# Powers of two of weight blocks from sums of squares on ScalarE in place of maxima on VectorE, asked for earlier

## The chip, the core and the metric

The kernel runs on one core of a Trainium2 chip. Its engines each work through a queue of their own, in order: TensorE (PE in the profile; PEld is its weight load), VectorE (DVE), ScalarE (ACT), GpSimd (POOL) and SyncE (SP), which here issues most of the transfers between the memory of the chip and the core. The metric is the time of one execution in microseconds of the device (us); lower is better.

## What is computed

A decoder block: normalisation, attention and a convolution side by side, gates, a projection, and then a SwiGLU feed-forward network (FFN) on 1024 tokens of width 1024 with a hidden width of 2816. The change concerns the FFN's first matrix:

```python
def swiglu_ffn(h, w_ffn_in, w_ffn_out):
    gate, up = jnp.split(h @ w_ffn_in, 2, axis=-1)
    return (jax.nn.silu(gate) * up) @ w_ffn_out
...
        x = x + rms_norm(merged @ w_mix_out[l], g_post_mix[l])
        h = rms_norm(x, g_pre_ffn[l])
        x = x + rms_norm(swiglu_ffn(h, w_ffn_in[l], w_ffn_out[l]), g_post_ffn[l])
```

## The kernel before

Every product is made in three passes, each operand split into a high and a low part (high x high, high x low, low x high). In the FFN's first matrix both parts are 16-bit floats, so a weight block has to be brought into their range first, by a power of two. `peaks` (line 122) finds the largest absolute value of each row of a block with DVE (L128), or of the two blocks of a pair, and joins them (L130, tile `pb`). `scales` (L133) sums these 128 values over the partitions with a one-column matmul against ones (L137), copies the sum (L140), keeps only its exponent (`power`, L120), and makes from it the factor `w` for the weights (L142, L143) and the factors `u` and `-u` that undo it in the results (L144, L145). With `w`, ACT casts the block to the high part (L239) and DVE makes the low part (L240); both are called from `quarters` or `part`.

The FFN has 22 hidden tiles of 128, each with a gate block and an up block of 128 x 1024 weights (`w_fi`). The first two tiles (`PLAIN`, in `ffn_half`) are computed in the plain way, four blocks with 24 matmuls of 512 columns for each half of the tokens. The other 20, j = 2 to 21, are pairs: `winograd` (L389) makes gate and up together in seven products (A11, A12, S2, S1, S3, S4, A22 of the weights) of 12 matmuls, 84 in all. After three matmuls comes a `tick`; a pair has 28. Three PSUM banks take the sums: X gets A11, is copied out (ACT, L398), gets S2 added, is copied out again (ACT, L403), and later gets S3 and A22 added; Z gets A12; V gets S1, is copied (ACT, L408), and gets S4. DVE joins these (L1816, L1821, L1825, L1829, L1838), and `sums` makes from two hidden tiles the Winograd sums for the next matrix and stores them (L1689 to L1701, transfers L1682): one difference and two stores at the end of an even tile, three and more at the end of an odd one.

While pair j is multiplied, the blocks of pair j+1 are prepared. `pair` (L337) writes this down in ticks from the pair's start: at LD = 2 SP issues the load of the two blocks (tiles `d` and `b`), at PK = 11 come `peaks`, at SC = 14 `scales`, at PC = 18, 20, 26 the first three of six `quarters`; the rest follow at 1, 8 and 10 in the next pair (8: casts of S3 and S4; 10: cast of A22). All engines take these steps into their queues at the place where they are called.

In the stage before, the projection `w_mx` (L1657) runs over eight token tiles, each followed by a residual and a norm (`residual`, `mix_norm`: squares L1344 and L1366, roots L1331, DVE L1351 and L1355, the normed tile L1368); four normed tiles are transposed (L1376). The pieces of work on the plain blocks stand in a list, of which one piece is done in every PIECE ticks; `weights` (L310) loads and lists blocks ahead, by `ahead` one further, and does at once what is still missing of the block that it hands out. 

Of the kernel before, what the change touches and what calls it, by code (L numbers as in the profile page):

```python
# [20 lines left out]
KT = 8  # L21
# [16 lines left out]

LD, PC = 2, (18, 20, 26)

PK, SC = 11, 14

TINY, W_TOP, H_TOP = 1e-22, 4096.0, 128.0

FIRST = 4

# [23 lines left out]
class Build:  # L70
# [51 lines left out]
    def peaks(self, i):  # L122

        nc = self.nc
        m = self.tiny(2, "pk", 4)
        raws = [self.raw[i - 1], self.raw[i]] if self.jobs[i][2] == "row2" else [self.raw[i]]
        for c, r in enumerate(raws):
            nc.vector.tensor_reduce(m[:, c:c + 1], r, AX.X, OP.max, apply_absolute_value=True)  # L128
        p = self.tiny(1, "pb", 4, BF16)
        nc.vector.scalar_tensor_tensor(p, m[:, 0:1], TINY, m[:, len(raws) - 1:len(raws)], op0=OP.max, op1=OP.max)  # L130
        self.peak[i] = p

    def scales(self, i):  # L133

        nc = self.nc
        ps = self.bank("s")
        nc.tensor.matmul(ps[:, 0:1], self.ones16, self.peak.pop(i), start=True, stop=True)  # L137
        t = self.tiny(4, "sc", 6)
        a, w, u, n = (t[:, c:c + 1] for c in range(4))
        nc.vector.tensor_copy(a, ps[:, 0:1])  # L140
        self.power(a, a)
        nc.vector.reciprocal(w, a)  # L142
        nc.vector.tensor_scalar(w, w, W_TOP, None, op0=OP.mult)  # L143
        nc.vector.tensor_tensor(u, a, self.unscale, op=OP.mult)  # L144
        nc.vector.tensor_scalar(n, u, -1.0, None, op0=OP.mult)  # L145
        self.scale[i] = w, u, n


    def bg(self, g):
# [102 lines left out]
    def quarters(self, i, c):  # L252


        nc = self.nc
        if c == 0:
            self.hl[i] = {}
        o = self.hl[i]
        r1, r2 = self.raw[i - 1], self.raw[i]
        a11, a12, a21, a22 = r1[:, :H], r1[:, H:], r2[:, :H], r2[:, H:]  # L260
        add = self.wsplit.tensor_tensor
        l, r = slice(0, H), slice(H, 2 * H)
        sw = self.scale[i][0] if i >= self.scaled else None
        if c == 0:
            h, w = self.both(r1, sw)
            o["A11"], o["A12"] = (h[:, l], w[:, l]), (h[:, r], w[:, r])
        elif c == 1:
            self.s12 = self.ring()
            add(self.s12[:, l], a21, a22, op=OP.add)
            add(self.s12[:, r], self.s12[:, l], a11, op=OP.add)  # L270
        elif c == 2:
            h, w = self.both(self.s12, sw)
            o["S1"], o["S2"] = (h[:, l], w[:, l]), (h[:, r], w[:, r])
        elif c == 3:
            self.s34 = self.slot()
            add(self.s34[:, l], a11, a21, op=OP.add)
            add(self.s34[:, r], self.s12[:, r], a12, op=OP.add)
# [59 lines left out]
    def pair(self, i):  # L337
# [8 lines left out]
        if n < len(J) and J[n][2] == "row1":  # L346
            todo += [(LD, lambda: self.load_ahead(n + 1))]
            if n >= self.scaled:
                todo += [(PK, lambda: self.peaks(n + 1)), (SC, lambda: self.scales(n + 1))]
            todo += [(k, lambda c=c: self.quarters(n + 1, c)) for c, k in enumerate(PC)]  # L350
            if self.conv_sums:
                todo.append((22, self.channel_sum))
            self.queued = n + 2
# [1035 lines left out]
    def norm_scale(self):  # L1389

        nc = self.nc
        self.ones16 = self.small.tile([128, 128], BF16, name="ones16")
        nc.vector.memset(self.ones16, 1.0)
        g = self.row_gain(self.g_pref_row)
        t = self.small.tile([128, 3], F32, name="nsc")
        a, b, self.unscale = (t[:, c:c + 1] for c in range(3))
# [6 lines left out]
        nc.vector.tensor_scalar(self.unscale, a, 1 / (H_TOP * W_TOP), None, op0=OP.mult)  # L1403
# [10 lines left out]
def build(ctx, tc, aps):  # L1414
    B = Build(ctx, tc, aps)
# [229 lines left out]
    for tiles in ((0, 1), (2,), (3,), (4,), (5,), (6,), (7,)):  # L1645
        banks = {tt: (B.bank(), B.bank()) for tt in tiles}
        for kt in range(KT):
            if len(W) == kt:
                B.ahead = int(kt < KT - 1)
                W.append(B.weights(mx[kt]))  # L1650
            for tt in tiles:
                m = mop[tt // 4]
# [22 lines left out]
        B.finish(e)  # L1675


    B.PIECE = 4
    held = {}

    def spill(p, name, x):
# [365 lines left out]
```

## Time and profile before

| | |
|---|---|
| median of three runs (lowest, highest) | 1740.39 us (1739.18, 1743.83) |
| the profiled execution | 1745.37 us |
| its span in the profile | 1743.6 us |
| DVE's maxima L128 | 44, each 1.21 us |
| PE's one-column matmuls L137 | 24, each 0.16 us |

Times in the profile are counted from the start of the span. A row of the order in time gives start, duration, engine, line, operation, output<-input by the program's names without numbers (`b`, `c`, `d` are buffers, `p` is PSUM, `sc` and `pb` the small tiles of the scales), and in brackets how long the engine was idle before it and who released it. A matmul's duration holds its way through the array, so neighbours overlap; what counts is the distance from start to start. SPq marks a transfer that SP issues, with the time to issue it.

### The profile page before, as it was taken

The page shows a single profiled execution, that of the slowest core. Times are in us where ns is not written, and L with a number is a line of the kernel's source. Part 1 is how long each engine was busy: PE and PEld are TensorE (multiplying, and loading weights), DVE is VectorE, ACT ScalarE, POOL GpSimd, SP SyncE. Part 2 cuts the span into 40 slices and gives each one's busy share as a digit, 9 for nine tenths or more (in the row PEclk, how much of TensorE's full clock was granted, in tenths as well). Part 3 has the DMA queues.
Part 4 walks back from the last instruction along what each step waited for, and adds up shares of the span by engine and source line. Part 5 has one row for each costly group of instructions (what it writes and reads, how often), then busy time and mean ns, then how long its engine had stood idle before and what let it go on. Part 6 is the DMA issues. An engine that isn't in the chain of part 4 may idle for free.

```text
span 1743.6 us, 24779 instructions
## 1 busy us (share of the span) xinstructions
PE 1692.8 (97%) x8722; PEld 1287.1 (74%) x8722; DVE 1317.8 (76%) x2438; ACT 806.4 (46%) x1552; POOL 494.9 (28%) x386
## 2 busy tenths in 40 slices
PE   8999999999999999999999999889999999999998
PEld 7788888888888999999888887434444444488886
DVE  6789988889997656686764855777777777767586
ACT  6343444343444566677622446633333333454453
POOL 0018778788884245455200300000000000000000
PEclk9999999999999999999999999999999999999999
DMA  4342434445678696878746722112332232394244
GB/s 162 112 170 91 151 124 138 161 170 174 189 180 225 211 286 175 226 222 235 242 169 228 267 76 82 67 73 91 119 117 91 91 126 92 133 355 159 89 147 151
DMA packets 159625, 277.58 MB, mean 159 GB/s; under 512 B 47009, under 2 KB 78428, under 8 KB 159500
## 3 DMA queue, kind: packets, MB, share of 16 engines
q1 hardware_dynamic: 155292, 263.82, 46.7%
q0 software_dynamic: 3920, 11.91, 2.1%
q8 instruction: 69, 1.13, 0.3%
q14 instruction: 56, 0.46, 0.1%
q10 hardware_dynamic: 288, 0.27, 0.0%
HBM read 185.34 MB, written 95.33 MB: 161 GB/s over the span
## 4 chain that ended last, share of the span: by engine, by line
PE 79%; DVE 10%; DMA 4%; ACT 3%; issue 2%; POOL 1%; SPq 0%; DVEq 0%; ACTq 0%; POOLq 0%
PE p L1930 12%; PE p L384 12%; PE p L385 12%; PE p L386 12%; PE p L1657 5%; PE p L368 4%; PE p L372 4%; PE p L370 4%; DVE pk L128 2%; PE p L1005 2%; PE p L1003 2%; PE p L1007 2%; PE p L617 2%; PE p L1101 2%; PE p L1137 1%
## 5 line engine op out<-in xcount | busy, mean ns | idle before, releaser
L384 PE MATMUL p<-b,b 128*128 128x512 f32 (+1 forms) x1124 | 433.9, 386 | 0.9 <-ACT c L398 0.7
L385 PE MATMUL p<-b,b 128*128 128x512 f32 (+1 forms) x1124 | 433.6, 386 | 0.0
L386 PE MATMUL p<-b,b 128*128 128x512 f32 (+1 forms) x1124 | 433.5, 386 | 0.0
L1930 PE MATMUL p<-b,b 128*128 128x512 f32 x924 | 209.8, 389 | 0.0
L1930 PEld LDWEIGHTS p<-b,b 128*128 128x128 f32 x924 | 173.4, 188 | 36.1
L747 DVE SCALAR_TENSOR_TENSOR p<-b,par,p 128x511 f32<-128x511 f32 (+14 forms) x232 | 163.4, 738 | 0.0
L368 PE MATMUL p<-b,b 128*128 128x512 f32 (+1 forms) x368 | 147.0, 399 | 0.0
L372 PE MATMUL p<-b,b 128*128 128x512 f32 (+1 forms) x368 | 146.4, 398 | 0.0
L370 PE MATMUL p<-b,b 128*128 128x512 f32 (+1 forms) x368 | 146.2, 397 | 0.0
L384 PEld LDWEIGHTS p<-b,b 128*128 128x128 f32 x644 | 120.9, 188 | 26.4 <-ACT c L403 0.7
L386 PEld LDWEIGHTS p<-b,b 128*128 128x128 f32 x644 | 120.9, 188 | 25.1
L385 PEld LDWEIGHTS p<-b,b 128*128 128x128 f32 x644 | 120.9, 188 | 24.9
L249 POOL TENSOR_TENSOR b<-d,b 128x1024 fp32r<-128x1024 f32 x44 | 106.8, 2428 | 79.9 <-ACT b L248 72.5
L1003 PE MATMUL p<-b,b 128*128 128x256 f32 x384 | 116.0, 302 | 0.0
L1005 PE MATMUL p<-b,b 128*128 128x256 f32 x384 | 115.2, 300 | 0.0
L1007 PE MATMUL p<-b,b 128*128 128x256 f32 x384 | 115.1, 300 | 0.0
L384 PEld LDWEIGHTS <-b 128*128 128x128 f16 x480 | 47.1, 98 | 75.6 <-issue 21.9
L1243 DVE TENSOR_TENSOR b<-c,b 128x512 fp32r<-128x512 f32 (+1 forms) x101 | 70.4, 698 | 35.3 <-ACT b L1242 35.0
L1242 ACT CAST b<-b 128x512 fp32r<-128x512 f32 (+1 forms) x117 | 72.3, 619 | 47.3 <-PE p L1930 18.0
L1243 DVE TENSOR_TENSOR b<-b,b 128x512 fp32r<-128x512 f32 (+1 forms) x117 | 80.0, 688 | 17.7 <-ACT b L1242 15.8
L386 PEld LDWEIGHTS <-b 128*128 128x128 f16 x480 | 47.2, 98 | 57.5 <-issue 1.4
L1657 PE MATMUL p<-b,b 128*128 128x512 f32 x384 | 89.6, 392 | 0.0
(272 smaller groups left out, 3526.1 us busy)
## 6 DMA issues: line engine op xcount, KB each, us to landing
b<-w_in SPq DMA_DIRECT2D x30, 512.0 KB, 4.8
dk<-c SPq DMA_DIRECT2D x48, 256.0 KB, 3.0
dq<-c SPq DMA_DIRECT2D x48, 256.0 KB, 3.7
b<-dq SPq DMA_DIRECT2D x48, 256.0 KB, 8.7
b<-dk SPq DMA_DIRECT2D x48, 256.0 KB, 6.2
b<-w_fi SPq DMA_DIRECT2D x24, 512.0 KB, 4.9
d<-w_in SPq DMA_DIRECT2D x23, 512.0 KB, 3.8
dqS<-c SPq DMA_DIRECT2D x44, 256.0 KB, 2.0
```

What stands on the lines that cost most here:

```text
L368: nc.tensor.matmul(ps, hi[:, s], a, start=kt == 0, stop=False)
L370: nc.tensor.matmul(ps, hi[:, s], b, start=False, stop=False)
L372: nc.tensor.matmul(ps, lo[:, s], a, start=False, stop=kt == nk - 1)
L384: nc.tensor.matmul(ps, hi[:, s], a, start=first and kt == 0, stop=False, skip_group_check=True)
L385: nc.tensor.matmul(ps, hi[:, s], b, start=False, stop=False, skip_group_check=True)
L386: nc.tensor.matmul(ps, lo[:, s], a, start=False, stop=kt == 3, skip_group_check=True)
L747: nc.vector.scalar_tensor_tensor(A[i][:, j:], src[i][:, :H - j], w[i], A[i][:, j:], op0=OP.mult, op1=OP.add)
L1003: nc.tensor.matmul(o, a, hi[:, s], start=kt == 0, stop=False)
L1005: nc.tensor.matmul(o, a, lo[:, s], start=False, stop=False)
L1243: nc.vector.tensor_tensor(s[:, 512:512 + n], src, f(s[:, :n]), op=OP.subtract)
L1657: nc.tensor.matmul(banks[tt][nh], st, wt[:, nh * H:(nh + 1) * H], start=bool(kt == 0 and a), stop=bool(kt == KT - 1 and b))
L1930: nc.tensor.matmul(acc[t], x, y, start=first and e == 0, stop=last and e == 2, skip_group_check=True)
```

## The change

`peaks` no longer takes maxima on DVE: ACT squares each block (times 2^-13) with the sum of each row as a by-product, into a tile that nobody reads (`junk`), and adds the two sums of a pair, or copies the one. The one-column matmul stays. `scales` then shifts the bits of the sum right by one and keeps the exponent, which halves the exponent (the power of two of a root), and makes `w`, `u` and `-u` in four small DVE operations instead of six. The steps in a pair come at other ticks: `peaks` at 9 instead of 11, `scales` at 16 instead of 14, and the three `quarters` at 19, 17, 25 instead of 18, 20, 26, so that the sums on DVE (quarter 1) go ahead of the first cast (quarter 0). For the plain blocks `ahead` is always 1, and PIECE is 2 instead of 4 until the pairs begin.

```diff
-PK, SC = 11, 14
-TINY, W_TOP, H_TOP = 1e-22, 4096.0, 128.0
+PK, SC, PS = 9, 16, (19, 17, 25)
+TINY, W_TOP, H_TOP = 2.0 ** -60, 2.0 ** -13, 128.0
...
         for c, r in enumerate(raws):
-            nc.vector.tensor_reduce(m[:, c:c + 1], r, AX.X, OP.max, apply_absolute_value=True)
+            nc.scalar.activation(self.junk, r, AF.Square, scale=W_TOP, accum_out=m[:, c:c + 1])
         p = self.tiny(1, "pb", 4, BF16)
-        nc.vector.scalar_tensor_tensor(p, m[:, 0:1], TINY, m[:, len(raws) - 1:len(raws)], op0=OP.max, op1=OP.max)
+        if len(raws) == 2:
+            nc.scalar.activation(p, m[:, 0:1], AF.Identity, bias=m[:, 1:2])
+        else:
+            nc.scalar.copy(p, m[:, 0:1])
...
-        nc.vector.tensor_copy(a, ps[:, 0:1])
-        self.power(a, a)
+        nc.vector.tensor_scalar(a.bitcast(I32), ps[:, 0:1].bitcast(I32), 1, 0x7F800000,
+                                op0=OP.logical_shift_right, op1=OP.bitwise_and)
+        nc.vector.tensor_scalar(a, a, 2.0 ** 64, TINY, op0=OP.mult, op1=OP.max)
         nc.vector.reciprocal(w, a)
-        nc.vector.tensor_scalar(w, w, W_TOP, None, op0=OP.mult)
-        nc.vector.tensor_tensor(u, a, self.unscale, op=OP.mult)
-        nc.vector.tensor_scalar(n, u, -1.0, None, op0=OP.mult)
-        self.scale[i] = w, u, n
+        nc.vector.tensor_scalar(u, self.unscale, a, None, op0=OP.mult)
+        self.scale[i] = w, t[:, 2:3], t[:, 3:4]
...
-            todo += [(k, lambda c=c: self.quarters(n + 1, c)) for c, k in enumerate(PC)]
+            todo += [(k, lambda c=c: self.quarters(n + 1, c)) for c, k in enumerate(PS if n >= self.scaled else PC)]
...
-                B.ahead = int(kt < KT - 1)
+                B.ahead = 1
...
-        B.ahead = 0
...
-    B.PIECE = 4
+    B.PIECE = 2
...
+    B.PIECE, B.ahead = 4, 0
```

In the changed file the lines behind L130 have other numbers: L131 and L133 are the new add and copy, L140 is the one-column matmul, L241 and L242 are the casts and low parts (L239 and L240 before).

The first place is ACT's queue in one pair (j = 4), from the first copy of X to the copy of V. Before (`c` on the left are the copies of PSUM, `b` and `c` with `sc` on the right are casts of weights):

```order
L398 COPY c_11882<-p_11880 128x512
L239 ACTIVATE b_11917<-b_11888,sc_11807 128x1024
L239 ACTIVATE c_11927<-b_11751,sc_11807 128x512
L403 COPY c_11883<-p_11880 128x512
L1818 ACTIVATE c_11882<-c_11882,sc_11807 128x512
L408 COPY c_11884<-p_11942 128x512
```

and after the change:

```order
L398 COPY c_11870<-p_11868 128x512
L241 ACTIVATE b_11905<-b_11876,sc_11803 128x1024
L128 ACTIVATE junk,pk_11912<-d_11882 128x1024
L128 ACTIVATE junk,pk_11912<-b_11884 128x1024
L131 ACTIVATE pb_11915<-pk_11912 128x1
L241 ACTIVATE c_11920<-b_11741,sc_11803 128x512
L403 COPY c_11871<-p_11868 128x512
L1820 ACTIVATE c_11870<-c_11870,sc_11803 128x512
L408 COPY c_11872<-p_11930 128x512
```

The two squares of the next pair's blocks and their sum have come between the cast for S3 and S4 and the cast for A22, ahead of the second copy of bank X (L403).

The second place is PE's queue around the one-column matmul of the same pair, with the engines that each row waits for. Before (V is `p_11942`, X is `p_11880`):

```order
L137 MATMUL p_11950<-pb_11936,ones_10348 128x1 [waits DVE_49]
L384 LDWEIGHTS b_11859
L384 MATMUL p_11942<-b_11476,b_11859 128x512
L385 LDWEIGHTS b_11859
L385 MATMUL p_11942<-b_11476,b_11859 128x512
```

and after (V is `p_11930`, X is `p_11868`):

```order
L386 MATMUL p_11930<-b_11498,b_11844 128x512
L140 LDWEIGHTS ones_10349
L140 MATMUL p_11944<-pb_11915,ones_10349 128x1 [waits Activation_49]
L384 LDWEIGHTS b_11905
L384 MATMUL p_11868<-b_11529,b_11905 128x512 [waits Activation_49]
```

Before, it stood in the middle of the product S1 into V; now it stands at that product's end, and the next matmul is the first of S3 into bank X, which waits for ACT.

The third place is ACT's queue at the plain blocks, around the norm of the last token tile (L1366 to L1368) and the transposed tokens (L1382). Before:

```order
L1707 ACTIVATE c_11135<-p_11136,sc_10493 128x512
L1366 ACTIVATE b_11196,ss_11197<-d_11140 128x1024
L1331 ACT_TABLE_LOAD
L1331 ACTIVATE rr_11199<-ss_11197,eps_rms 128x1
L1368 ACTIVATE b_11196<-d_11140,rr_11199 128x1024
L239 ACTIVATE b_11216<-b_11113,sc_11184 128x512 x2
L239 ACTIVATE b_11255<-b_11115,sc_11248 128x512 x2
L1382 ACTIVATE b_11273<-p_11268,gain_10403 128x512
```

and after:

```order
L241 ACTIVATE b_11183<-b_10500,sc_11170 128x512 x2
L1708 ACT_TABLE_LOAD
L1708 ACTIVATE c_11137<-p_11138,sc_10495 128x512
L1366 ACTIVATE b_11201,ss_11202<-d_11142 128x1024
L1331 ACT_TABLE_LOAD
L1331 ACTIVATE rr_11204<-ss_11202,eps_rms 128x1
L1368 ACTIVATE b_11201<-d_11142,rr_11204 128x1024
L128 ACTIVATE junk,pk_11215<-b_11131 128x1024
L133 CAST pb_11217<-pk_11215 128x1
L241 ACTIVATE b_11238<-b_11131,sc_11227 128x512 x2
```

The casts of the third plain block have gone ahead of the norm's L1366, and the square and copy for the fourth block stand right behind L1368. In PE's queue the one-column matmuls of the third and fourth block now stand 12 and 36 matmuls into the plain products, where the last three stood 0, 24 and 48 matmuls in.

More of the change, by code (lines that the diff above doesn't have):

```diff
@@ L138, in scales @@
         t = self.tiny(4, "sc", 6)
-        a, w, u, n = (t[:, c:c + 1] for c in range(4))
-        nc.vector.tensor_copy(a, ps[:, 0:1])
-        self.power(a, a)
+        a, w, u = t[:, 0:1], t[:, 1:2], t[:, 2:4]
+        nc.vector.tensor_scalar(a.bitcast(I32), ps[:, 0:1].bitcast(I32), 1, 0x7F800000,
+                                op0=OP.logical_shift_right, op1=OP.bitwise_and)
+        nc.vector.tensor_scalar(a, a, 2.0 ** 64, TINY, op0=OP.mult, op1=OP.max)
         nc.vector.reciprocal(w, a)
-        nc.vector.tensor_scalar(w, w, W_TOP, None, op0=OP.mult)
-        nc.vector.tensor_tensor(u, a, self.unscale, op=OP.mult)
-        nc.vector.tensor_scalar(n, u, -1.0, None, op0=OP.mult)
-        self.scale[i] = w, u, n
+        nc.vector.tensor_scalar(u, self.unscale, a, None, op0=OP.mult)
+        self.scale[i] = w, t[:, 2:3], t[:, 3:4]
     def bg(self, g):
@@ L255, in quarters @@
         nc = self.nc
-        if c == 0:
-            self.hl[i] = {}
-        o = self.hl[i]
+        o = self.hl.setdefault(i, {})
         r1, r2 = self.raw[i - 1], self.raw[i]
@@ L1391, in norm_scale @@
         nc = self.nc
+        self.junk = self.small.tile([128, 1024], BF16, name="junk")
         self.ones16 = self.small.tile([128, 128], BF16, name="ones16")
@@ L1394, in norm_scale @@
         g = self.row_gain(self.g_pref_row)
-        t = self.small.tile([128, 3], F32, name="nsc")
-        a, b, self.unscale = (t[:, c:c + 1] for c in range(3))
+        t = self.small.tile([128, 4], F32, name="nsc")
+        a, b, self.unscale = t[:, 0:1], t[:, 1:2], t[:, 2:4]
         yield 8
@@ L1402, in norm_scale @@
         nc.vector.tensor_scalar(b, b, H_TOP, None, op0=OP.mult)
-        nc.vector.tensor_scalar(self.unscale, a, 1 / (H_TOP * W_TOP), None, op0=OP.mult)
+        for c in range(2):
+            nc.vector.tensor_scalar(t[:, 2 + c:3 + c], a, (1 - 2 * c) / H_TOP, None, op0=OP.mult)
         self.gain2 = self.small.tile([128, 8], F32, name="gain2")
```

## The prediction

> **What bounds the kernel now.** I read the page first, then the view of waits for TensorE (PE), then the order in time around those waits.
>
> ```profile
> span 1743.6 us, 24779 instructions
> PE 1692.8 (97%) x8722; PEld 1287.1 (74%) x8722; DVE 1317.8 (76%) x2438; ACT 806.4 (46%) x1552; POOL 494.9 (28%) x386
> ```
>
> PE is busy for 97% of the span, so only time in which PE stands still, or runs at a lower clock, can be won. The view of waits (PE's line <- who released it: us in total, times, longest) says for whom it stands still:
>
> ```profile
> PE p L137 <- DVE pb L130: 28.3, 21, 5.5
> ```
>
> L137 is the one-column matmul that sums a block's peaks over the partitions. It stands in PE's queue among the large matmuls, so these wait with it until VectorE (DVE) has found the maxima. 28.3 us of such waits is 1.6% of the span, and the change works on just these. How they look in time is seen in two neighbouring hidden tiles (a "pair" below is one of the 20 passes of the Winograd loop; j=9, odd, then j=10, even):
>
> ```profile
> 1279.35 0.38 PE L384 MATMUL p<-b,b 128*128 128x512 f16 x1
> ...
> 1288.20 0.38 PE L386 MATMUL p<-b,b 128*128 128x512 f16 x1
> 1288.91 0.16 PE L137 MATMUL p<-pb,ones 128*128 128x1 bf16 x1 [0.33 <-DVE pb L130]
> 1288.94 0.38 PE L384 MATMUL p<-b,b 128*128 128x512 f16 x1
> ...
> 1298.00 0.38 PE L384 MATMUL p<-b,b 128*128 128x512 f16 x1
> ...
> 1306.85 0.38 PE L386 MATMUL p<-b,b 128*128 128x512 f16 x1
> 1308.53 0.16 PE L137 MATMUL p<-pb,ones 128*128 128x1 bf16 x1 [1.30 <-DVE pb L130]
> 1308.56 0.38 PE L384 MATMUL p<-b,b 128*128 128x512 f16 x1
> ...
> 1317.62 0.38 PE L384 MATMUL p<-b,b 128*128 128x512 f16 x1
> ```
>
> From 1279.35 to 1288.20 are 41 steps, 0.216 us each: 84 matmuls make 18.13 us. The odd pair takes 18.65 us, the even one 19.62: they lose 0.52 and 1.49, all at L137 (0.74 and 1.71 us from matmul to matmul, less one step). A stop costs 0.19 us more than the wait that is shown.
>
> **The change part by part: the pairs.** Of the waits, 16.0 us belong to the 18 pairs j=3 to 20, by this row less 5.47 and 5.32 us for two that are quoted below:
>
> ```profile
> PE p L137 <- DVE pb L130: 26.8, 20, 5.5
> ```
>
> (stretch from 1100 us on). With 18 x 0.19 us for the stops that is 19.4 us. DVE loses its two maxima and ScalarE (ACT) gets two squares with a sum; the one-column matmul moves from 14 ticks to 16 ticks after the pair's start (a tick is three matmuls, 0.65 us). Whether PE still waits depends on when the weight block lands, since the squares are asked for at tick 9, before it is there:
>
> ```profile
> 1301.03 0.32 SPq L1682 DMA_DIRECT2D dqS<-c  x1
> 1301.94 0.40 SPq L215 DMA_DIRECT2D b<-w_fi  x1
> 1281.97 0.40 SPq L215 DMA_DIRECT2D b<-w_fi  x1
> b<-w_fi SPq DMA_DIRECT2D x18, 512.0 KB, 4.7
> ```
>
> The last row is the list of DMA issues (count, size, median us to landing). In an even pair the load stands in SyncE's (SP) queue behind the stores of the last sums, which wait for DVE (the store at 1301.03 for L1701): it is issued 3.94 us after the pair's start and lands at 3.94 + 4.7 = 8.64. In an odd pair it is issued at 2.62 and lands at 7.32. The diff moves none of this, and DVE's last sums follow PE's last products as before.
>
> New durations by the nearest rows: a square with a sum over 128x1024 exists at L1366, a one-column add at L1331, and the two operations that come next in ACT's queue are old ones (idle time left as printed):
>
> ```profile
> 1076.56 1.06 ACT L1366 ACTIVATE b<-d 128x1024 f32<-128x1024 f32 x1 [3.52 <-DVE d L1355]
> 1077.74 0.30 ACT L1331 ACTIVATE rr<-ss,eps_rms 128x1 f32<-128x1 f32 x1
> 1302.30 1.15 ACT L239 ACTIVATE b<-b,sc 128x1024 f16<-128x1024 f32 x1 [0.92 <-DVE b L277]
> 1303.35 0.71 ACT L239 ACTIVATE c<-b,sc 128x512 f16<-128x512 f32 x1
> 1306.03 0.58 ACT L403 COPY c<-p 128x512 f32<-128x512 f32 x1 [1.97 <-PE p L386]
> 1306.51 0.72 ACT L1818 ACTIVATE c<-c,sc 128x512 f32<-128x512 f32 x1
> ```
>
> Even pair, in us from its start: second square starts at 8.67 (0.03 for the semaphore), its sum is there 1.15 later (L1366 starts at 1076.56, the operation on its sum at 1077.74, less 0.03): 9.82. The add, like L1331, ends 0.33 later: 10.15. PE sees it 0.06 later, an estimate from the 0.03 of other hand-overs: 10.21. The matmul's own turn is 16 ticks = 48 steps = 10.36. So **the wait for the peak goes**. But behind the squares in ACT's queue stand the cast of A22 (L239, 0.71) and the copy of bank X (L403, 0.58), which was done by 1306.61 - 1298.00 = 8.61 so far. PE's next product after the one-column matmul, S3, adds into the same bank X and has to wait for that copy. ACT's instructions overlap by 0.10 (1306.03 + 0.58 against 1306.51): the cast starts at 10.05, the copy at 10.66, it ends at 11.24, PE goes on at 11.30 instead of 10.39. **A new wait of 0.91 us takes the place of 1.49.** Odd pair: all of it 1.32 us earlier, 9.98 against 10.39: no wait, 0.52 won.
>
> That ACT keeps its order is seen above: the cast at 1303.35, whose input and scale were old, did not pass the L239 ahead of it that waited 0.92 us for DVE. The Trainium skill says so too ("TensorE: Matmul & The Clock Gate", section Architectural detail: the queues of ScalarE and VectorE are strictly first in, first out); by that the 0.91 us stay, and without it the first rival below would be the likelier one. No row speaks against it.
>
> Nine even pairs keep 9 x 0.91 = 8.2 us. Some blocks land late: these two lines of the chain of work (start, us) are 1.9 and 0.3 us over the median, the first in an odd pair:
>
> ```profile
> 1242.57 6.58 DMA b<-w_fi
> 1455.32 5.01 DMA b<-w_fi
> ```
>
> The first gives 9.98 + 1.9 - 10.39 = 1.5 us, the second 0.3 more. Together 10 us stay of 19.4: **9.4 us won.** Bounds: all 19.4, and below nothing (slower rival). DVE's half of A22 waits for the cast too, to 11.5, and the small scale steps behind it; what these feed is wanted only at the next pair's start at 18.1, so the wait is covered. DVE's relief (two maxima, two small steps) wins nothing in the pairs, where DVE is not what PE waits for once the peak is ACT's.
>
> **The first pair, j=2.** DVE is behind here, with the sums for the Winograd operands:
>
> ```profile
> 1141.98 0.38 PE L384 MATMUL p<-b,b 128*128 128x512 f16 x1 [0.70 <-ACT c L398]
> 1144.38 0.60 ACT L1242 CAST b<-b 128x512 f16<-128x512 f32 x1
> 1151.49 0.19 PE L137 MATMUL p<-pb,ones 128*128 128x1 bf16 x1 [5.47 <-DVE pb L130]
> 1151.92 0.63 PE L385 MATMUL p<-b,b 128*128 128x512 f16 x1
> 1157.40 0.38 PE L386 MATMUL p<-b,b 128*128 128x512 f16 x1
> ```
>
> PE loses 0.89 + 5.66 us (0.70 and 5.47 with 0.19 each), and after the long stop it runs at half speed: from 1151.92 to 1157.40 are 13 matmuls, 0.42 us each, 0.21 too much: 2.7 us. In all 9.2. The block has landed long before, so ACT can square it after the cast at 1144.38, from 1144.9 on; the second square starts at 1145.95, PE goes on 2.63 us later (the sum above) at 1148.6. Its turn without waits is about 1146.3 (it began its 42nd matmul at 1145.64 with 0.89 lost; seven steps more and 0.03, less 0.89). So at worst 2.3 us stay, if DVE and ACT are no sooner; none if they are 2.4 us sooner (two maxima of DVE are gone ahead of it, partly into idle time). I take 1.7: **7.5 us won**, between 6.9 and 9.2, a half-speed stretch not being due after so short a stop: after 1.30 us there is none (1308.53 to 1308.56).
>
> **The unpaired blocks** (two hidden tiles ahead of the pairs). Here the last token tile's norm stands in the same queues.
>
> ```profile
> 1084.65 0.57 ACT L1344 ACTIVATE d<-p 128x512 f32<-128x512 f32 x1
> 1089.22 0.18 PE L137 MATMUL p<-pb,ones 128*128 128x1 bf16 x1 [1.48 <-DVE pb L130]
> 1094.68 1.15 ACT L1368 ACTIVATE b<-d,rr 128x1024 f32<-128x1024 f32 x1 [0.87 <-DVE rr L1336]
> 1099.92 0.16 PE L137 MATMUL p<-pb,ones 128*128 128x1 bf16 x1 [5.32 <-DVE pb L130]
> 1102.46 0.73 PE L1376 MATMUL p<-ident,b 128*128 128x128 f32 x4
> 1103.03 0.38 PE L368 MATMUL p<-b,b 128*128 128x512 f16 x1
> ```
>
> After the change the square of the fourth block stands in ACT's queue behind L1368, the norm's last step. L1344, the norm's first step, can start when the last tile's matmuls are done, at about 1082.5 (the casts that stood ahead of it are made earlier), 2.15 us sooner. Into this come the third block's square and copy (1.15 + 0.33) and, between the norm's steps, its scale steps (four small ones, 0.7 by my estimate). The norm's end therefore stays where it is, L1368 at about 1094.7. Its successor starts 1.05 later; square 1.15 and copy 0.33: PE can go on at 1097.3. But its one-column matmul now stands 12 matmuls further ahead: 36 matmuls after 1082.4, at about 1090.4. **PE stands 6.9 us instead of 1.48 + 5.32 in two stops.** Half speed lasted from 1099.92 to 1103.03 there and from 1151.49 to 1157.3 in the first pair, 3.1 to 5.8 us, half of it lost: 1.5 to 2.9. The transposes, 18 matmuls on, then start at 1097.3 + 3.9 + (1.5 to 2.9) = 1102.7 to 1104.1, against 1102.46 and 0.36 us of slow transposes: 0 to 1.4 us lost, I take **0.7 lost**. The price of longer standing is bounded below by nothing and above by 2.9.
>
> The Trainium skill ("TensorE: Matmul & The Clock Gate", The HAM clock gate) has the clock halved after an idle window of about 3.4 us, and freed after as much work. The rows agree in kind (0.42 us steps after 5.3 and 5.5 us, none after 1.3); its 3.4 us would make this loss 1.7 us, an estimate, inside the 1.5 to 2.9.
>
> The rest costs nothing: ahead of this, two blocks' squares go to ACT, which is busy for less than half of the span, and one load goes ahead of the token loads, under matmuls that wait for nothing.
>
> **Sum.** 9.4 + 7.5 - 0.7 = 16.2 us. The profiled execution took 1745.37 us (span 1743.6 and 1.8 around it), the median of the runs is 1740.39; from that, **1724.2 us**, 0.93% less.
>
> **Rivals.**
> 1. *All waits of the pairs go*, because the copy of X is not late (a sooner landing by 0.9 us, from stores that clear sooner). Then 19.4 + 9.2 - 0.7 = 27.9: 1712.5 us. For it: the odd pairs have 0.4 us to spare already. Against: SP's load waits for DVE's last sum, which waits for PE.
> 2. *The peak's wait is only traded* for an equal one: blocks land 0.5 to 0.7 us later than the median. At 0.5, 9 x 1.41 + 9 x 0.09 + 1.8 = 15.3 stay and 4.1 are won, at 0.7 0.5; with 7.5 in the first pair and -2.9 in the unpaired blocks that is 8.7 to 5.1: 1732 to 1735 us. For it: the spread of the landings. Against: nothing new is transferred in the pairs.
> 3. *Slower*: the same wait on ACT, but at the late landing's price. While ACT waits for a block it holds the copy of X, which DVE's maxima never did. Landing x us later costs 9 (0.91 + x) in even pairs and 9 (x - 0.41) in odd ones. It eats 19.4 + 7.5 - 0.7 us from x = 1.2 on. If every block came as late as the one of 6.58 us (x = 1.9), 9 x 2.81 + 9 x 1.49 = 38.7 us of waits stand against 19.4: 1740.4 + 19.3 - 6.8 = 1753 us. For it: one block of 18 did. Against: the other 17.
> 4. *It does not do what it says*: the one-column matmul still waits as long, for ACT instead of DVE, in the first pair too. Then about 1740 us.
>
> **How the numbers follow.** Forecast 0.58 (1719 to 1730 by its own bounds), rival 1 0.17, rival 2 0.14, rival 3 0.05, rival 4 0.06. The likeliest gives the time. The range leaves out rivals 3 and 4 and the last of the first: 1711 to 1736. 0.3%, 5.2 us, is about what a measurement of this kernel can tell from no change. Faster by more than that: forecast, rival 1, and half of rival 2 and a little, 0.83; within it 0.11; slower 0.06.
>
> **What would show it.** In the changed profile: PE waits at S3's first matmul (L384) for ACT's copy L403, 0.9 us in even pairs and none in odd ones; next to none at the one-column matmul in the pairs; one stop of 6 to 7 us ahead of the transposes with slow matmuls behind it, and 1 to 2 us in the first pair. Odd pairs take 18.1 us, even ones 19.0. It is wrong if odd pairs stop too, if ACT's squares take more than 1.3 us each, or if the unpaired blocks' stop is over.

## The result: 0.73% less, and where it came from

| | before | after |
|---|---|---|
| median (lowest, highest), 5 runs each | 1740.39 us (1737.62, 1744.52) | 1727.75 us (1726.10, 1731.05) |
| ratio after / before, 95% interval | | 0.9927 [0.9906, 0.9948] |
| the profiled execution | 1745.37 us | 1729.81 us |
| its span | 1743.6 us | 1728.0 us |

In a later set of runs the changed kernel stood at 0.9916 [0.9902, 0.9930]. The page of the changed kernel, and its view of waits for PE (line, who released it: us in total, times, longest):

```profile
span 1728.0 us, 24733 instructions
PE 1692.5 (98%) x8722; PEld 1289.3 (75%) x8722; DVE 1256.7 (73%) x2323; ACT 860.4 (50%) x1664; POOL 495.8 (29%) x386
```

```profile
PE p L384 <- ACT c L403: 7.8, 11, 0.9
PE p L140 <- ACT pb L133: 6.1, 1, 6.1
...
PE p L1376 <- ACT b L1368: 1.7, 1, 1.7
...
PE p L384 <- DVE c L1823: 0.7, 1, 0.7
```

PE's busy time is what it was; its waits got shorter. The 28.3 us behind DVE's peak (L130) are gone, and four others stand there: for the copy of X (L403) in the pairs, for one square of a plain block (L133), in the projection for the norm's last step (L1368), and once, in the first pair, for DVE's L1823. Stage by stage, from the starts of PE's rows in the two profiled executions (us):

| stage | before | after | won |
|---|---|---|---|
| up to the projection | 990.98 | 991.00 | 0.0 |
| projection | 91.15 | 93.34 | -2.2 |
| plain hidden tiles | 53.80 | 54.29 | -0.5 |
| first pair, j=2 | 27.52 | 19.95 | 7.6 |
| the 19 pairs behind it | 363.67 | 353.00 | 10.7 |
| the second matrix, to the end | 216.48 | 216.45 | 0.0 |

**An odd and an even pair** in the changed kernel's order in time (start, duration, engine, line; in brackets the idle time before and the releaser), j=9 and j=10 as before:

```profile
1270.56 0.38 PE L384 MATMUL p<-b,b 128*128 128x512 f16 x1
...
1280.92 0.17 PE L140 MATMUL p<-pb,ones 128*128 128x1 bf16 x1
1280.95 0.38 PE L384 MATMUL p<-b,b 128*128 128x512 f16 x1
...
1288.71 0.38 PE L384 MATMUL p<-b,b 128*128 128x512 f16 x1
...
1299.08 0.17 PE L140 MATMUL p<-pb,ones 128*128 128x1 bf16 x1
1300.07 0.38 PE L384 MATMUL p<-b,b 128*128 128x512 f16 x1 [0.82 <-ACT c L403]
...
1307.83 0.38 PE L384 MATMUL p<-b,b 128*128 128x512 f16 x1
```

The odd pair takes 18.15 us, which is all matmuls. In the even one the one-column matmul no longer waits, and 19.12 us are left because the first matmul of S3 does. ScalarE's queue in the even pair shows for what:

```profile
1296.15 1.06 ACT L128 ACTIVATE junk<-d 128x1024 bf16<-128x1024 f32 x1 [2.05 <-DMA d<-w_fi]
...
1297.46 1.06 ACT L128 ACTIVATE junk<-b 128x1024 bf16<-128x1024 f32 x1 [0.16 <-DMA b<-w_fi]
...
1298.64 0.30 ACT L131 ACTIVATE pb<-pk 128x1 bf16<-128x1 f32 x1
1298.84 0.71 ACT L241 ACTIVATE c<-b,sc 128x512 f16<-128x512 f32 x1
1299.45 0.56 ACT L403 COPY c<-p 128x512 f32<-128x512 f32 x1
```

ACT stands twice for the landing of a block, then squares, adds and casts, and only then copies X, although the product that it copies was over by 1296.65. PE goes on 0.06 us after the copy's end.

**The projection.** On ACT, at the first token tile's norm and at the end of the fourth one's, and on PE at the transposes of these four:

```profile
1012.15 1.04 ACT L128 ACTIVATE junk<-b 128x1024 bf16<-128x1024 f32 x1
...
1013.32 0.19 ACT L133 CAST pb<-pk 128x1 bf16<-128x1 f32 x1
1013.42 0.59 ACT L1344 ACTIVATE d<-p 128x512 f32<-128x512 f32 x1
...
1048.04 1.15 ACT L1368 ACTIVATE b<-d,rr 128x1024 f32<-128x1024 f32 x1 [0.87 <-DVE rr L1336]
```

```profile
1049.23 0.33 PE L1376 MATMUL p<-ident,b 128*128 128x128 f32 x1 [1.68 <-ACT b L1368]
```

The square of the second plain block, now asked for one block ahead, stands in front of a norm's first step, and its scale steps and casts stand between later ones. ACT and DVE pass these norms to and fro, one tile behind the other, and nothing takes the delay up: the fourth tile's last step starts at 1048.04, where the kernel before has it at this time,

```profile
1045.74 1.15 ACT L1368 ACTIVATE b<-d,rr 128x1024 f32<-128x1024 f32 x1 [0.87 <-DVE rr L1336]
```

and its transposes wait 1.68 us.

**The plain tiles.** The one stop, and ScalarE's queue at its end:

```profile
1092.15 0.38 PE L372 MATMUL p<-b,b 128*128 128x512 f16 x1
1098.66 0.16 PE L140 MATMUL p<-pb,ones 128*128 128x1 bf16 x1 [6.13 <-ACT pb L133]
1098.69 0.59 PE L368 MATMUL p<-b,b 128*128 128x512 f16 x1
...
1103.34 0.45 PE L372 MATMUL p<-b,b 128*128 128x512 f16 x1
1103.62 0.38 PE L368 MATMUL p<-b,b 128*128 128x512 f16 x1
```

```profile
1096.20 1.15 ACT L1368 ACTIVATE b<-d,rr 128x1024 f32<-128x1024 f32 x1 [0.87 <-DVE rr L1336]
1097.26 1.04 ACT L128 ACTIVATE junk<-b 128x1024 bf16<-128x1024 f32 x1
...
1098.42 0.19 ACT L133 CAST pb<-pk 128x1 bf16<-128x1 f32 x1
```

The fourth block's square comes behind the norm's last step, and from 1098.69 on, PE makes a step in 0.43 us instead of 0.216 for almost 5 us.

### The profile page after: what moved, and what is told of

It reads as the page before. It is cut to its first block, busy times and chain, and to the rows that moved or that the text cites. A ratio compares the mean times of both kernels' runs of the same rounds, so it can differ in the third digit from the quotient of the medians.

```text
span 1728.0 us, 24733 instructions
## 1 busy us (share of the span) xinstructions
PE 1692.5 (98%) x8722; PEld 1289.3 (75%) x8722; DVE 1256.7 (73%) x2323; ACT 860.4 (50%) x1664; POOL 495.8 (29%) x386
## 4 chain that ended last, share of the span: by engine, by line
PE 82%; DMA 5%; DVE 5%; ACT 5%; issue 2%; POOL 1%; SPq 0%; DVEq 0%; ACTq 0%; POOLq 0%
PE p L384 13%; PE p L385 13%; PE p L386 13%; PE p L1932 12%; PE p L368 4%; PE p L372 4%; PE p L370 4%; PE p L1659 3%; DMA b<-w_fi 2%; PE p L1005 2%; PE p L1007 2%; PE p L1003 2%; PE p L617 2%; PE p L1101 2%; PE p L1137 1%
```

## The experiments

Twelve more runs were made (the last is the changed kernel again), in three sets, each with the kernel before on the same chip (its medians: 1742.0, 1743.17, 1742.5 us). The stretch ahead of the projection is the same code in all of them, and yet in the profiled executions it took between 983.6 and 993.3 us. So the readings below go by the stages behind it; the ratio stands beside them. These readings are of one execution each. The same kernel (after and e12) took 353.00 and 353.86 us in its 19 pairs.

| kernel | projection | plain tiles | first pair | 19 pairs | ratio to before, 95% interval |
|---|---|---|---|---|---|
| before | 91.15 | 53.80 | 27.52 | 363.67 | |
| after | 93.34 | 54.29 | 19.95 | 353.00 | 0.9927 [0.9906, 0.9948] |
| e1_copy_first | 93.37 | 54.06 | 20.77 | 370.11 | 1.0018 [1.0005, 1.0031] |
| e2_maxima_tick16 | 91.14 | 54.90 | 25.05 | 346.63 | 0.9903 [0.9885, 0.9922] |
| e3_old_pieces | 91.15 | 51.07 | 21.39 | 355.92 | 0.9906 [0.9887, 0.9924] |
| e4_old_ticks | 93.35 | 54.12 | 19.92 | 355.88 | 0.9938 [0.9921, 0.9956] |
| e5_pairs_late | 93.35 | 53.88 | 19.86 | 356.78 | 0.9940 [0.9926, 0.9954] |
| e6_pool_loads | 93.34 | 53.43 | 19.95 | 344.74 | 0.9866 [0.9846, 0.9885] |
| e7_front | 91.16 | 53.91 | 19.95 | 356.37 | 0.9909 [0.9891, 0.9928] |
| e8_both | 91.14 | 53.89 | 19.86 | 356.79 | 0.9928 [0.9912, 0.9944] |
| e9_before_pool | 91.15 | 54.92 | 26.39 | 362.32 | 0.9997 [0.9986, 1.0008] |
| e10_pool_old_pieces | 91.15 | 51.37 | 21.39 | 344.73 | 0.9846 [0.9829, 0.9864] |
| e11_pool_mx | 91.15 | 56.17 | 19.96 | 344.73 | 0.9867 [0.9852, 0.9881] |
| e12_after_again | 93.35 | 54.49 | 19.96 | 353.86 | 0.9916 [0.9902, 0.9930] |

### Squares behind the copy of X (e1)

```diff
-PK, SC, PS = 9, 16, (19, 17, 25)
+PK, SC, PS = 13, 16, (19, 17, 25)
```

> The kernel after the change, with the squares of the next pair asked for at tick 13 instead of 9, so that in ScalarE's queue they stand behind the second copy of bank X (L403) and no longer ahead of it; the one-column matmul stays at tick 16. Theory A (the new wait of PE in even pairs comes only from that place in the queue; the block is not later than before): the copy ends at 8.6 us after the pair's start, the squares begin as soon as the block lands (8.3 to 9.0), their sum is there at 9.9 to 10.6 against a turn at 10.4, so 0 to 0.2 us are left in even pairs. The changed kernel's waits at L384 for L403 in the pairs (6.7 us in 9 pairs, with 0.19 for each stop 8.4 us) go: 1727.75 - 8.4 + 1 = about 1720 us, even pairs 18.2 to 18.4 us. Rival B (the landing is what PE waits for, by whatever way): the wait moves to the one-column matmul L140 or, by the copy of bank V that now stands behind the squares, to the first matmul of S4, and even pairs stay at 19.0: 1727 us.

Neither: 1746.31 us, 0.2% slower than the kernel before, and every pair from the second on, odd or even, takes 19.57 us. ScalarE's queue in the even pair j=10 (start 1296.84), and PE behind it:

```profile
1304.81 0.58 ACT L403 COPY c<-p 128x512 f32<-128x512 f32 x1 [1.97 <-PE p L386]
1305.29 0.72 ACT L1820 ACTIVATE c<-c,sc 128x512 f32<-128x512 f32 x1
1305.92 1.04 ACT L128 ACTIVATE junk<-d 128x1024 bf16<-128x1024 f32 x1
...
1307.08 1.06 ACT L128 ACTIVATE junk<-b 128x1024 bf16<-128x1024 f32 x1
...
1308.26 0.30 ACT L131 ACTIVATE pb<-pk 128x1 bf16<-128x1 f32 x1
...
```

```profile
1308.61 0.16 PE L140 MATMUL p<-pb,ones 128*128 128x1 bf16 x1 [1.25 <-ACT pb L131]
```

The copy of X is on time and L403 is gone from the pairs' waits, as theory A said. But the expectation began the squares at the landing. Nothing in these rows waits for a landing: both squares now stand behind the copy and a Silu (L1820), where in the changed kernel the first is done before the second block is there. 3.8 us of work from the copy's start make 11.77 us after the pair's start, against a turn at 10.36.

### Maxima kept, only the ticks changed (e2)

```diff
-PK, SC = 11, 14
+PK, SC, PS = 11, 16, (19, 17, 25)
...
-            todo += [(k, lambda c=c: self.quarters(n + 1, c)) for c, k in enumerate(PC)]
+            todo += [(k, lambda c=c: self.quarters(n + 1, c)) for c, k in enumerate(PS if n >= self.scaled else PC)]
```

> The kernel before the change (maxima on VectorE, six small steps, old pieces), with only the ticks of the changed kernel behind the maxima: scales at 16 instead of 14, quarters at 19, 17, 25; maxima stay at 11. Theory A (in the pairs it is the later turn of the one-column matmul that wins the time, not the engine that makes the peak): in an even pair of the kernel before, the matmul ran at 10.53 us after the start and in an odd one at 9.56, against a turn that now comes at 10.4: odd pairs 18.15 us, even ones 18.2 to 18.5. 19.4 us of losses shrink to 2 or 3; the first pair's long wait shrinks by the 1.3 us of the later turn. 1740.4 - 17 - 1.3 = about 1722 us, so ahead of the change itself. Rival B (the move to ScalarE wins it): VectorE's six small steps and the first cast come 1.3 us later, the low parts behind them miss the next pair's start, and the waits come back there: 1735 us or more.

1725.55 us, theory A. The 19 pairs win 17.0 us, more than the 10.7 of the change itself: odd pairs take 18.15 us, even ones 18.32. Its view of waits from the second pair on has no row for PE. Over the whole kernel its ratio, 0.9903, and that of the change, 0.9927, have overlapping intervals. The first pair keeps its wait of 4.2 us and takes 25.05 us.

### The edits to the plain blocks' queue undone (e3)

```diff
-                B.ahead = 1
+                B.ahead = int(kt < KT - 1)
...
         B.PIECE = 3
+        B.ahead = 0
...
-    B.PIECE = 2
+    B.PIECE = 4
```

> The kernel after the change without its edits to the plain blocks' queue: one piece in 4 ticks again, and no block ahead on the last input tile of the projection. Theory A (these edits cost what the prediction had put at nothing): the squares of the second plain block no longer stand among ScalarE's norm steps of the fourth token tile, the 2.0 us that the transposes of the first four tiles waited go, and the stop of 6.1 us for the fourth block becomes one of 4.5 to 5.8 us: 1727.75 - 2 - 1 = about 1725 us (1723 to 1727). Rival B (the edits are what keeps the waits down to one stop): two stops again as before the change, 1730 us or more.

1727.14 us, at the edge of theory A's range, with one stop and not rival B's two. By its ratio it cannot be told from the changed kernel, so the stages have to say it. The projection is back at 91.15 us, the wait for L1368 is gone, the stop is 3.92 us long (the fourth block's one-column matmul has its turn 48 matmuls into the plain products again, instead of 36) and the plain tiles take 3.2 us less than after. The first pair takes 1.4 us more (its blocks are prepared later). The 19 pairs took 2.9 us more: 1.9 of them in one odd pair (j=7, 20.05 us), whose second square could start only 9.68 us after the pair's start instead of at about 7.3: PE waited 0.69 us for the peak and 0.92 for the copy. That is the price of a late landing that the third rival had named, in one pair of 19. It is there only without the block ahead on the last input tile, though why is not shown: in the five profiles without that block whose loads SP issues (before, e2, e3, e7, e8), transfers still run at 15 to 26 GB/s between 7.4 and 9.0 us after the start of j=7; in the five with it (after, e1, e4, e5, e12) none do. So these edits cost 5.4 us ahead of the pairs and give back 1.4 in the first and 1.9 in j=7.

### Squares with the old ticks (e4)

```diff
-PK, SC, PS = 9, 16, (19, 17, 25)
+PK, SC, PS = 11, 14, (18, 20, 26)
```

> The kernel after the change with the pair's old ticks: squares at 11, scales at 14, quarters at 18, 20, 26. It is ScalarE's squares without the new moments. Theory A: an even pair's peak is there at 10.2 us after the start as in the changed kernel, but the one-column matmul's turn is at 9.06: a wait of 1.15 us and 0.19 for the stop in nine even pairs; the copy of X is done before PE gets to S3, so the wait at L403 goes; odd pairs (peak at 8.9) wait for nothing. Even pairs 19.45 us instead of 19.1, odd 18.15; the first pair loses 1.3 us more: 1727.75 + 9 x 0.4 + 1.3 = about 1732.5 us. Rival B (the engine decides, the ticks are worth nothing): 1727 to 1728.5 us.

1731.43 us, theory A. From the second pair on there is one row of waits for PE,

```profile
PE p L140 <- ACT pb L131: 9.7, 9, 1.4
```

nine times in nine even pairs, and odd ones take 18.15. The first pair, 19.92 us, loses nothing by the old ticks; there the expected 1.3 us was wrong.

### Squares late and scales late (e5)

```diff
-PK, SC, PS = 9, 16, (19, 17, 25)
+PK, SC, PS = 13, 19, (20, 17, 25)
...
-        sw = self.scale[i][0] if i >= self.scaled else None
+        sw = self.scale[i][0] if i >= self.scaled and c != 1 else None
```

> The kernel after the change with squares at tick 13, as in the run with squares at 13 and scales at 16, but with scales at 19 and the quarters at 20, 17, 25. That earlier run's matmul ran at 11.77 us after the start of every pair, odd or even, early or late landing: copy of X (from 8.0), the Silu on the first sum (L1820), two squares and the add, one behind the other, 3.8 us. Theory A (that chain is all there is to it, and what comes behind the scale has time to spare): with its turn at 19 ticks = 12.31 us the matmul waits for nothing, the copy of X is not held, all pairs take 18.15 us: 8.4 us less than the changed kernel in nine even pairs, 1727.75 - 8.4 = about 1719.5 us. Rival B: the scale is now known 2 us later, the casts and low parts for the next pair come too late, and PE waits at the first product of the next pair (L384 or L386 for L241 or L242): 1725 us or more.

1734.14 us, in rival B's range, but at a place it did not name. From the second pair on the one-column matmul waits for nothing, and all these pairs take 18.82 us:

```profile
PE p L384 <- DVE c L1823: 9.2, 18, 0.5
```

```profile
1305.20 1.28 DVE L242 SCALAR_TENSOR_TENSOR b<-d,sc,b 128x1024 f16<-128x1024 f32 x1 [1.09 <-ACT b L241]
1306.40 0.68 DVE L1823 TENSOR_TENSOR c<-p,c 128x512 f32<-128x512 f32 x1
```

(The second edit lets quarter 1, the sums on DVE at tick 17, run before the scale is there; it does not use it.) The first row counts the pairs from the second on, the others are DVE's order in one of them. The first low part (L242) waits for a cast that waits for the scale, and holds up L1823, which reads bank X; the last product (A22) may add into X only after that. The scale cannot come as late as tick 19 while L1823 stands behind that low part.

### Loads from GpSimd's queue (e6)

```diff
-            self.nc.sync.dma_start(self.raw[j][:, :n], src)
+            (q or self.nc.sync).dma_start(self.raw[j][:, :n], src)
...
-            todo += [(LD, lambda: self.load_ahead(n + 1))]
+            todo += [(LD, lambda: self.load_ahead(n + 1, nc.gpsimd if n >= self.scaled else None))]
```

> The kernel after the change, with the loads of the next pair's blocks issued from GpSimd's queue instead of SyncE's, at the same tick 2. Theory A (in even pairs the blocks land 1.3 us later only because their load stands behind the stores of the last sums in SyncE's queue, and this landing is what holds the copy of X): loads are issued at 1.3 to 2.6 us in odd and even pairs alike, land at or under 7.5, even pairs take 18.15 us like odd ones, 1727.75 - 8.4 = about 1719.5 us. Rival B (it is not the place in SyncE's queue that makes them late, but buffers that come free late, or the stores' traffic): landing stays at 8.3 to 9.0 in even pairs and these stay at 19.0: 1727 us.

1720.44 us, theory A's time, and every pair from the second on takes 18.15 us; PE waits for nothing there. Two pieces of its order in time, GpSimd from the pair ahead on and ACT in the even pair j=10, which starts at 1285.71:

```profile
1270.98 0.53 POOL L217 DMA_DIRECT2D d<-w_fi  x1 [15.79 <-ACT c L398]
...
1290.46 0.53 POOL L217 DMA_DIRECT2D d<-w_fi  x1 [18.43 <-issue]
```

```profile
1291.00 1.04 ACT L128 ACTIVATE junk<-d 128x1024 bf16<-128x1024 f32 x1
...
1292.17 1.06 ACT L128 ACTIVATE junk<-b 128x1024 bf16<-128x1024 f32 x1
...
1294.16 0.56 ACT L403 COPY c<-p 128x512 f32<-128x512 f32 x1
```

The load at 1290.46 is for the next pair's squares; that at 1291.00 reads what was asked for at 1270.98, 20.0 us sooner. The expected 1.3 to 2.6 us was too late by a pair: GpSimd's queue has nothing else to do here and does not stay with PE's ticks. ACT no longer waits for a landing, and the copy of X starts at 8.45 us instead of 10.74.

### Another order on the plain blocks (e7), and both (e8)

```diff
-                B.ahead = 1
+                B.ahead = int(kt < KT - 1)
...
-    B.PIECE = 2
+    B.PIECE, B.ahead = 1, 1
...
         Ws.append((B.weights(fi[j][0]), B.weights(fi[j][1])))
+        if j == 0:
+            q, nop = list(B.pieces), (0, lambda: None)
+            B.pieces = deque((q[0], q[4], nop, nop, q[1], q[2], q[3], *q[5:]))
         ffn_half(j, 0, Ws[j])
+        B.PIECE = 2
```

> The kernel after the change, with another order of the work on the plain blocks and nothing else: no block ahead on the last input tile of the projection (as before the change), and at the start of the plain hidden tiles the squares of the third and fourth block first, one piece per tick, ahead of the last token tile's norm in ScalarE's queue, the scales from the fifth tick on. Theory A (the long stop is there because the fourth block's square stands behind the norm's last step L1368, and the wait in the projection because the second block's square stands among the norm steps): both go, with them the half-speed matmuls behind the stop; the norm ends one or two us later, which the transposes do not notice. 2.2 us of the projection, 6.3 us of stop and 2.3 us of half speed: 1727.75 - 10.8 = about 1717 us. Rival B (that norm is what PE waits for in the end): the stop moves to the transposes L1376, which wait for L1368 or its copies, and no more than 3 or 4 us are won: 1724 us.

1728.2 us; the ratio is 0.9909, against 0.9927 for the change in its own set. Rival B: the projection's 2.2 us are won, the stop for the fourth block is gone, and the plain tiles still take 53.91 us:

```profile
PE p L1376 <- ACT b L1368: 4.6, 1, 4.6
```

The transposes now wait for the last token tile's norm, which the squares and casts ahead of it have held up: its last step L1368 starts 16.6 us after the projection's last matmul, 4.7 us later than after the change. (The late landing in j=7, 20.01 us, takes back 1.9 us in this run's pairs, as in e3.) What PE waits for at this place is that norm, whichever instruction is the first to stand behind it. The second edit together with e5's:

> Both: squares at tick 13, scales at 19 and quarters at 20, 17, 25 in the pairs, and the new order on the plain blocks. Theory A of both holds and they add up, since the stages follow each other: 1727.75 - 8.4 - 10.8 = about 1708.5 us, 1.8% under the kernel before. If only one of them holds, 1717 to 1720 us.

1730.27 us. Its first stages are those of e7 and its pairs those of e5, to 0.1 us: they add up, as expected, but neither part brought what had been expected of it.

### The kernel before with loads from GpSimd's queue (e9)

The edit is that of e6, on the kernel before.

> The kernel before the change (maxima on VectorE, old ticks, old pieces), with the loads of the next pair's blocks issued from GpSimd's queue, as in the run that did this to the changed kernel, where they went out as soon as a buffer came free, about a pair ahead. It splits the 19.4 us that the pairs lost before. Theory A: 1.3 us of the late landing in each even pair goes, and the late one of the 18 loads; what an odd pair lost (0.52 us) stays in all, since VectorE's own order (low parts of the last blocks, then the maxima) lets the peak be ready 0.3 us after the turn at tick 14: 18 pairs of 18.65 us, 19.4 - 18 x 0.52 = 10 us won, 1743 - 10 = about 1732 us. Rival B (all of the loss is the landing): 18.15 us in all pairs, 1723 us. Rival C (VectorE's order alone): nothing won, 1742 us.

1741.81 us, no change: rival C. The pairs wait as they did (14.7 us in 18 pairs for the peak; the 1.3 us less than before are the two late landings, in j=7 and j=18). DVE in the even pair j=10, which starts at 1292.87, and two rows of the odd one ahead of it, which starts at 1274.21:

```profile
1281.19 1.21 DVE L128 TENSOR_REDUCE pk<-d 128x1 f32<-128x1024 f32 x1
...
1283.56 0.16 DVE L130 SCALAR_TENSOR_TENSOR pb<-pk 128x1 bf16<-128x1 f32 x1
```

```profile
1293.06 0.69 DVE L1694 TENSOR_TENSOR c<-c,c 128x512 f32<-128x512 f32 x1
1293.78 0.69 DVE L1696 TENSOR_TENSOR c<-c,c 128x512 f32<-128x512 f32 x1
...
1295.17 0.69 DVE L1701 TENSOR_TENSOR c<-c,c 128x512 f32<-128x512 f32 x1
...
1300.80 1.21 DVE L128 TENSOR_REDUCE pk<-d 128x1 f32<-128x1024 f32 x1
...
1303.18 0.16 DVE L130 SCALAR_TENSOR_TENSOR pb<-pk 128x1 bf16<-128x1 f32 x1
```

With the blocks long there, the maxima begin at 7.93 us in an even pair and at 6.98 in an odd one, since an even pair's DVE queue opens with the sums of the odd tile before it. These 0.95 us are the difference between the two waits (1.30 and 0.33), and the landing has no part in it.

### Two ways to put the best parts together (e10, e11), and the change again (e12)

e10 is e6 with e3's edits; e11 is e6 with these:

```diff
-                B.ahead = 1
+                B.ahead = int(kt < KT - 1)
...
-    B.PIECE = 2
+    B.PIECE, B.ahead = 2, 1
```

> The changed kernel with the loads from GpSimd's queue in the pairs and the plain blocks' queue as before the change (one piece in 4 ticks, no block ahead on the last input tile). Theory A (stages follow each other, so what the two runs with one of these edits showed adds up): the pairs all take 18.15 us; the projection takes 2.2 us less, the plain tiles 3.2 us less, the first pair 1.4 us more than in the changed kernel with these loads: 1720.4 - 4.0 = about 1716.5 us. Rival B (the stop only moves, as in the run with the squares ahead of the norm): 1719 us or more.

1716.22 us, theory A, the lowest median of all: 1.5% under the kernel before, and 12 us under the changed kernel of the same set (e12). Each stage is as in the run it was taken from, within 0.3 us.

> The changed kernel with the loads from GpSimd's queue in the pairs, and only one of its edits to the plain blocks' queue undone: no block ahead on the last input tile of the projection; behind it one piece in 2 ticks and one block ahead, as changed. Theory A (the wait for L1368 in the projection comes from that one block's square and copy among ScalarE's norm steps, and the stop for the fourth block from the pieces behind it): the projection takes 91.15 us as before the change instead of 93.35, the stop of 6.1 us and the first pair of 19.95 us stay: 1720.4 - 2.2 = about 1718 us. Rival B: the second block's work now comes at the start of the plain tiles and makes the long stop longer by as much: 1720 us.

1720.25 us, rival B. The projection is back at 91.15 us, so its loss does come from that one block; but the block's work now falls to the plain tiles, with a second wait there:

```profile
PE p L140 <- ACT pb L133: 8.1, 2, 6.2
```

> The changed kernel itself, on the same chip as the three others, as their common base. By its own runs 0.9927 of the kernel before: 1728 to 1731 us, with 0.9 us waits for L403 in even pairs again.

1728.34 us, as expected, with the waits at L403 (7.4 us in 9 pairs from the second on).

## Why the prediction came out

The sum was 16.2 us, and the two profiled executions differ by 15.56. The medians differ by 12.6 us in the first set and by 14.2 where e12 ran; the rest of the gap from 1724.2 to 1727.75 lies within what the stretch ahead of the projection varies. That the sum came within 0.7 us of the profiled difference is in part luck: the pairs won 1.3 us more than forecast in this execution, and the projection lost 2.2 that the sum had at nothing. Term by term:

- **Pairs: 9.4 forecast, 10.7 measured.** The mechanism is the one named: waits of 0.5 to 0.9 us at S3's first matmul for the copy L403, in even pairs alone; odd pairs at 18.15 us. The size is off by the 1.8 us set aside for late landings, which this profile does not have. The larger part of them was for the late block of j=7. The sum had taken it over because the diff moves no load in the pairs; but that lateness is there only without the block ahead on the last input tile (see e3), and so the change took it away. That the landing decides is shown by e6, where an early one removes all of it; that ACT's order does is shown by e1, where the copy moved ahead is on time. e1 pays for it elsewhere: both squares then stand in a row behind the copy, and the peak comes too late.
- **First pair: 7.5 forecast, 7.6 measured.** 1.7 us was to stay and 1.8 did (19.95 against 18.15), but not for the peak: for the copy of X again, and for DVE's L1823.

```profile
1149.92 0.38 PE L384 MATMUL p<-b,b 128*128 128x512 f16 x1 [0.77 <-ACT c L403]
1155.99 0.38 PE L384 MATMUL p<-b,c 128*128 128x512 f16 x1 [0.73 <-DVE c L1823]
```

The peak was there 10.2 us after the pair's start, ahead of its turn; the forecast had it at 1148.6, 12.7 us after the start of that pair before. And the copy behind the squares was not in the sum. So the size is right by two errors that cancel, which is luck. And 1.4 of the 7.6 us come from the plain blocks' edits, not from the engine or the ticks: without them (e3) this pair takes 21.39 us.
- **Plain tiles: 0.7 lost forecast, 0.5 measured.** One stop of 6.13 us instead of 6.9 (the norm's last step came 11.9 us after the projection's last matmul, not the 12.55 of before that the sum had kept), and the slow stretch as priced (eleven steps with 0.21 us too much, 2.3 us). The fourth block does stand behind L1368. e7 adds what the prediction did not see: it is the norm that PE waits for, so taking the square out of its way moves the stop and wins nothing.
- **"The rest costs nothing": wrong, 2.2 us.** This step failed. ACT was taken as free because it is busy for half of the span; yet in the projection it works through norms in a row, and what came in between from 1012.15 on was a wait of PE at 1049.23. e3 and e11 show that the block ahead on the last input tile does it.

The prediction left one thing unsaid: why the even pairs had waited in the first place. The expectation of e9 took it to be the late landing, as in the changed kernel, and that fell: before the change it was DVE's own sums. So the change brought the pairs a new dependence. Squares on ACT, which is idle early enough, wait for the landing; maxima on DVE, which is busy until 7 or 8 us into the pair, did so only for the two late ones (waits of 1.48 us in j=7 and 1.53 in j=18).

And the gain has two sources that are not the same thing. The engine wins the first pair (e4: 19.92 us with old ticks, e2: 25.05 with maxima and the old plain blocks' queue), where DVE was far behind. In the other 19 pairs, the matmul's later turn alone won 17.0 us (e2), the squares alone 7.8 (e4), and both together 10.7 (9.8 in e12): the copy of X behind the squares takes back more than the earlier peak is worth.

## What to carry to other kernels

When work moves to an engine with time to spare, read what stands behind it in that engine's queue: an instruction that waits for a transfer makes everything behind it wait for that transfer, also a copy that frees a bank. Before a slow step is made faster, try to give its consumer a later turn; here, in the 19 pairs, that alone was worth more than the move (17.0 us against 7.8), for a few numbers in a table. And if loads and stores share a queue, look for the loads that stand behind stores which wait for the last results: another queue (here GpSimd's) took 8.3 us out of the pairs.

## What the runs showed of the hardware

A stop of PE of the same length was not followed by a half-speed stretch of the same length. In the kernel before and in e9, whose code is the same there, 5.32 and 5.33 us of wait were followed by slow steps for 2.8 and 5.1 us, which makes the 1.1 us between their plain tiles in the table; in e3 a stop of 3.92 us was followed by 1.1 us at full speed, and then by slow steps up to 1103.9, transposes among them. The granted clock in the traces shows how this comes about: it was 0.50 from 1099.3 to 1102.7 (before), from 1094.2 to 1101.0 (e9) and from 1100.4 to 1103.8 (e3), so for 3.4 or 6.8 us, beginning in the stop or behind it; what falls into the stop costs nothing more. The Trainium skill ("TensorE: Matmul & The Clock Gate", The HAM clock gate) says that the activity window is free-running and does not reset when a kernel starts, and the rows agree in that such a stretch has no fixed place behind the start of a stop. A price for such a stretch is good to about 1 us.
